# Layer 0's projection: when the second feature block's weights are loaded and split, which queue carries the modulation rows, and the form of the first modulation

## The chip, the cores and the metric

One core of a Trainium2 chip runs the whole kernel in one launch. The metric is the time of the launch in device microseconds (us); several launches of one kernel are timed and the median is taken. The engines are TensorE (PE in the rows; its weight loads are PEld), VectorE (DVE), ScalarE (ACT), GpSimd (POOL) and SyncE (SP), each with an instruction queue of its own that is worked off in order. DMAs are issued from such queues too, mostly SP's.

## The reference

Two layers over 1024 latent tokens and 256 context tokens of width 1024. Each layer modulates its input by rows that come from a condition vector (adaLN), runs an attention mixer, and then a gated FFN with a short convolution. Layer 0's projection, which matters here:

```python
m = split(silu(c) @ ada_w[l] + ada_b[l], 6)        # 6 modulation rows of 1024, for latent and context
h = x * (1 + m[1]) + m[0]
qa, ka, va, qb, kb, vb = split(h @ w_in, [512, 640, 768, 1280, 1792])
qa, ka = rms_norm per head, times gain, then axial rotary (latent tokens)
# group A: global attention; group B (qb, kb, vb, 8 heads each): neighbourhood attention
```

All is float32. A product is computed as three matmuls of a high and a low half (`mm3`): hi x hi, hi x lo, lo x hi.

## The kernel before

**Weights.** `load_in` brings a block of the weights from DRAM in loads of 512 KB into the pool `raw` (two buffers for the whole kernel) and calls `split`: ScalarE casts a tile to its high half (L99), VectorE subtracts for the low half (L100), both into a tile of the ring `ring` (12 slots). A block of 512 columns takes four loads and eight ring tiles, one for each 128 rows (k).

**First modulation** (`ada_first`, L141). While 8.4 MB of `ada_w` come in as 16 tiles `wt`, TensorE multiplies the two condition vectors with them, in pieces of 512 columns, into four PSUM banks; four strips of partitions hold partial sums that 32 small matmuls against the selector `sel` (L185; 16 in the code, each in two instructions) add up and turn into columns. Then `mod0` is built. x is loaded by `first_loads` behind the `wt` loads, then w_in, the rotary table `rope0` (L531) and the two gain rows (L138). `group(0, k)` transposes x (L512), applies the modulation on ScalarE (L514) and splits the result into the halves `hh` and `hl`.

**Token blocks** (`tok`): kA/vA, qA, then vB, with group by group of 24 matmuls for 128 tokens. Between them `conv_cols` loads rows of the convolution's weights into `rt` and transposes them to columns (L129), through the one bank `small`, which VectorE empties (L131). A generator `ada_items` (called by `bg`) is stepped in between as well: it loads modulation weights `araw`, accumulates them on VectorE (L215, L219) and sums them over the partitions with two matmuls (L309, L310).

**Feature blocks** (L684 on): `proj_feat` makes qB and then kB. For each of four f it takes three chunks of tokens (512, 512, 256), so twelve groups of 24 matmuls (L385 to L387) in each block. After each group `ev` evicts it (ScalarE and VectorE) to `qst`, stores it (L676), steps `bg(3)` and then `side`. `side` runs two parts of `ada_cols` one after the other: a part first issues its bias rows and its first load, then in eight steps loads the next 512 KB of layer 1's `ada_w` into `raw` (L274) and multiplies the one there into the bank `cols` (a set of eight matmuls, L289), then adds the bias (L299) and stores the rows to DRAM (L300). So the first part ends, and the second begins, in the tenth call, and two of the second part's sets lie in qB. kB's weights are loaded (L686) when qB's last group has been emitted.

After both blocks `mod_cols` (L692, L696) loads six rows each (two of the layer norm, four of modulation), transposes them to columns for `m1` and `m2`, and attention begins (L730).

**Order.** TensorE's instructions stand in the order of the code inside `manual_pe`. Those of the other engines, and all DMAs, are placed by a scheduler at build time, when it reckons that they are ready; at run time each queue keeps that order. A buffer that is taken again makes its writer wait for its last reader.

Of the kernel before, what the change touches and what calls it, by code (L numbers as in the profile page):

```python
# [36 lines left out]
class Kern:  # L37
# [66 lines left out]
    def load_in(self, w, c0, n, lo_eng=None):  # L104

        nc = self.nc
        wv = w.rearrange("(k p) n -> p k n", p=128)
        out = []
        g = 1024 // n
        for k0 in range(0, KT, g):  # L110
            r = self.t(self.raw, [128, g, n], "raw")
            nc.sync.dma_start(r, wv[:, k0 : k0 + g, c0 : c0 + n])
            for w2 in self.split([r[:, : g // 2], r[:, g // 2 :]], 512, lo_eng=lo_eng):
                v = w2.rearrange("p l (k n) -> p l k n", n=n)
                out += [(v[:, 0, k], v[:, 1, k]) for k in range(g // 2)]
        return out


    def cols(self, tp, ppool, rows, tag, pool=None):

        nc = self.nc
        n = sum(r.shape[0] for r in rows)
        rt = self.t(tp, [128, 128], "rt", bufs=3)
        o = 0
        for r in rows:
            nc.sync.dma_start(rt[o : o + r.shape[0], :], r)
            o += r.shape[0]
        ps = self.t(ppool, [128, 512], "small")
        nc.tensor.transpose(ps[:, :n], rt[:n, :], self.ident[:n, :n])  # L129
        ct = self.t(pool or self.cst, [128, n], tag)  # L130
        nc.vector.tensor_copy(ct, ps[:, :n])  # L131
        return ct
# [8 lines left out]
    def ada_first(self, loads):  # L141

        nc, io = self.nc, self.io
        with ExitStack() as es:
# [11 lines left out]
            ps = [self.t(pp, [128, 512], f"a{j}") for j in range(4)]  # L156
            for x in ps:
                nc.vector.memset(x, 0.0)
            ar = self.t(ap, [128, 2048], "ar")
            sel = self.t(ap, [128, 2], "sel")  # L160
            nc.vector.memset(sel, 0.0)
            for g in range(4):
                nc.vector.tensor_copy(sel[32 * g : 32 * g + 2], self.ident[:2, :2])
# [12 lines left out]
            loads()  # L176
            for j in range(4):
                d = ar[:, j * 512 : (j + 1) * 512]
                if j % 2:
                    nc.vector.tensor_copy(d, ps[j])  # L180
                else:
                    nc.scalar.copy(d, ps[j])
            pt = self.t(pp, [128, 512], "small")
            for j in range(16):
                nc.tensor.matmul(  # L185
                    pt[:, 2 * j : 2 * j + 2], ar[:, j * 128 : (j + 1) * 128], sel,
                    start=True, stop=True, skip_group_check=True,
                )
            m0 = self.t(self.cst, [128, 2, 8, 2], "mod0")
            nc.vector.tensor_add(  # L190
                m0.rearrange("p a k v -> p (a k) v"),
                pt[:, :32].rearrange("p (n v) -> p n v", v=2),
                ct[:, 16:32].unsqueeze(2).to_broadcast([128, 16, 2]),
            )
# [71 lines left out]
    def ada_cols(self, tp, bank, l, part):  # L266
# [11 lines left out]
        for c in range(4):  # L278
            b0 = part * D + c * 256
            nc.sync.dma_start(  # L280
# [187 lines left out]
    def l0_project(self):  # L468
# [11 lines left out]
        w = io["w_in0"]  # L480

# [9 lines left out]
        def first_loads():  # L491
            load_x(0, 0)
# [37 lines left out]
        rp = self.t(tab, [128, 8, 128], "rp")  # L530
        nc.sync.dma_start(rp, io["rope0"])  # L531
        gq = self.t(tab, [128, HD], "gq")
        gk = self.t(tab, [128, HD], "gk")
        self.bcast(gq, io["qg"][0])
        self.bcast(gk, io["kg"][0])
# [80 lines left out]
        with self.manual_pe():  # L616
# [32 lines left out]
            wb = None  # L649
            for t in range(NT):  # L650
                tok(t, wv, 512, ev_vb)
                bg(3)
# [7 lines left out]
        with ExitStack() as e3:  # L660
# [5 lines left out]
            side = (  # L666
                x for part in range(2)
                for x in self.ada_cols(colp, lambda: self.t(pc, [128, 512], "cols"), 1, part)
            )

            def ev_feat(dst, scale):
                def ev(f, t0, n, ps):
# [671 lines left out]
    def conv_cols(self, l, tp, pp):  # L1344
# [3 lines left out]
        c0 = self.cols(tp, pp, [cw[0], cw[1]], f"cc{l}0")  # L1348
        c1 = self.cols(tp, pp, [cw[2], cb], f"cc{l}1")
        return [c0[:, 0:NF], c0[:, NF:], c1[:, 0:NF], c1[:, NF:]]  # L1350
# [1037 lines left out]
```

## Time and profile before

| | us |
|---|---|
| median of 3 runs | 2991.7 (2990.74 to 2994.36) |
| profiled execution | 2995.48 |
| its span, first to last instruction | 2993.7 |
| busy: TensorE / VectorE / ScalarE / GpSimd | 2836.2 / 2046.6 / 1366.0 / 625.0 |
| share of the chain that ended last: TensorE / VectorE / DMA / ScalarE | 81% / 7% / 5% / 4% |
| mean granted clock of TensorE | 0.973 |

The page of the profile gives the busy time of each engine and the chain of work that ended last, followed back from the last instruction. A stretch of the span can be cut out: its busy times, the clock that TensorE was granted (1.00 is 2.4 GHz, 0.50 is 1.2 GHz) and the DMA engines' share. A timeline lists instructions in order of time: the start in us from the start of the span, the length, the engine (SPq is SP's DMA queue), the line, the tiles written and read, the count when several are merged, and in brackets the idle time before it and what ended that.

### The profile page before, as it was taken

What the parts mean: (1) busy time and instruction counts of PE and PEld (TensorE: products, weight loads), DVE (VectorE), ACT (ScalarE), POOL (GpSimd) and SP (SyncE); (2) the same over time, 40 slices, a digit from 0 to 9 for tenths busy, and PEclk for the clock granted to TensorE, in tenths of its full rate; (3) what the DMA queues carried; (4) which work ended last, traced back from release to release, by engine and by line L of the source; (5) the groups of instructions that cost most, each with busy time, mean ns of one, the idle gap of its engine ahead of it and who ended that gap; (6) DMA issues with size and microseconds to landing.
All of it is one profiled execution on the core that took longest, in us unless ns stands there. A gap on an engine that the chain in (4) does not pass through costs nothing.

```text
span 2993.7 us, 44874 instructions
## 1 busy us (share of the span) xinstructions
PE 2836.2 (95%) x16692; PEld 2291.7 (77%) x16692; DVE 2046.6 (68%) x3768; ACT 1366.0 (46%) x2595; POOL 625.0 (21%) x840
## 2 busy tenths in 40 slices
PE   8997899999999989999999988989997999999998
PEld 5875677777788978888888877766676788888886
DVE  4875266666578778888878655467776777777655
ACT  4221155567435654444553352167743545545330
POOL 2610033354450000000001013345543000000001
PEclk8998999999999999999999998999998999999999
DMA  7567521033557653333367526732154222224741
GB/s 256 154 214 231 169 81 35 17 101 113 159 150 239 211 161 104 109 106 116 106 231 275 167 75 215 205 102 64 60 162 160 76 80 83 80 85 156 266 146 73
DMA packets 348227, 418.58 MB, mean 140 GB/s; under 512 B 23128, under 2 KB 263032, under 8 KB 346472
## 3 DMA queue, kind: packets, MB, share of 16 engines
q1 hardware_dynamic: 330248, 361.30, 38.6%
q0 software_dynamic: 14864, 52.70, 5.0%
q8 instruction: 131, 2.15, 0.3%
q10 hardware_dynamic: 2896, 1.70, 0.2%
q14 instruction: 88, 0.72, 0.1%
HBM read 318.84 MB, written 96.80 MB: 139 GB/s over the span
## 4 chain that ended last, share of the span: by engine, by line
PE 81%; DVE 7%; DMA 5%; ACT 4%; issue 2%; POOL 1%; SPq 0%; ACTq 0%; POOLq 0%; DVEq 0%
PE y L1667 8%; PE q L1667 8%; PE x L1667 8%; PE d L385 5%; PE d L386 5%; PE d L387 5%; PE S L730 5%; PE v L1667 4%; PE mm L385 4%; PE mm L386 3%; PE mm L387 3%; PE pv L875 3%; PE T L861 3%; PE pv L835 2%; PE T L826 2%; PE o L387 2%
## 5 line engine op out<-in xcount | busy, mean ns | idle before, releaser
L754 POOL TENSOR_SCALAR P<-P,rin 128x640 f32<-128x640 f32 (+3 forms) x288 | 250.8, 875 | 350.4 <-DVE rin L753 315.9
L1566 DVE TENSOR_TENSOR w<-raw,w 128x512 fp32r<-128x512 f32 x308 | 208.8, 691 | 164.8 <-ACT w L1564 164.7
L385 PE MATMUL d<-w,w 128*128 128x512 f32 x704 | 275.2, 391 | 0.0
L387 PE MATMUL d<-w,w 128*128 128x512 f32 x704 | 274.4, 390 | 0.0
L386 PE MATMUL d<-w,w 128*128 128x512 f32 x704 | 274.4, 390 | 0.0
L99 ACT CAST w<-raw 128x512 fp32r<-128x512 f32 x276 | 160.9, 620 | 186.6 <-PE d L387 127.4
L100 DVE TENSOR_TENSOR w<-raw,w 128x512 fp32r<-128x512 f32 x260 | 170.4, 696 | 107.7 <-ACT w L99 105.4
L730 PE MATMUL S<-k,q 64*128 64x256 f32 (+2 forms) x1824 | 193.0, 338 | 17.5 <-DVE nm L2109 7.9
L1714 POOL DMA_DIRECT2D g<-cv x44 | 23.5, 533 | 870.0 <-DVE cv L1713 870.0
L751 ACT ACTIVATE P<-P,nm 128x641 f32<-128x641 f32 (+4 forms) x208 | 161.4, 777 | 82.9 <-DVE nm L2109 46.7
L1564 ACT CAST w<-raw 128x512 fp32r<-128x512 f32 x308 | 182.6, 621 | 15.2 <-DVE raw L1571 11.4
L730 PEld LDWEIGHTS S<-k,q 64*128 64x128 f32 x1824 | 136.2, 189 | 52.9 <-issue 17.6
L741 ACT COPY PT<-T 128x512 f32<-128x512 f32 (+1 forms) x250 | 134.1, 566 | 81.1 <-PE T L861 78.8
L387 PEld LDWEIGHTS d<-w,w 128*128 128x128 f32 x704 | 132.4, 188 | 27.9
L385 PEld LDWEIGHTS d<-w,w 128*128 128x128 f32 x704 | 132.6, 188 | 27.5
L386 PEld LDWEIGHTS d<-w,w 128*128 128x128 f32 x704 | 132.6, 188 | 27.1
L875 PE MATMUL pv<-PT,v 128*64 128x128 f32 x2016 | 134.7, 282 | 14.4 <-ACT PT L741 13.1
L1658 DVE TENSOR_TENSOR w<-raw,w 128x512 fp32r<-128x512 f32 x176 | 112.3, 686 | 52.0 <-ACT w L1657 51.9
L861 PE MATMUL T<-ident,P 128*128 128x128 f32 x1008 | 136.3, 282 | 12.0 <-POOL P L754 8.1
L1802 ACT COPY ug<-q 128x512 f32<-128x512 f32 x44 | 25.8, 587 | 254.8 <-PE q L1667 254.8
L875 PEld LDWEIGHTS pv<-PT,v 128*64 128x64 f32 x2016 | 110.6, 139 | 40.6 <-ACT PT L741 23.0
L1657 ACT CAST w<-raw 128x512 fp32r<-128x512 f32 x176 | 98.8, 618 | 87.2 <-PE d L387 70.1
(338 smaller groups left out, 7624.8 us busy)
## 6 DMA issues: line engine op xcount, KB each, us to landing
raw<-in_up_dram SPq DMA_DIRECT2D x132, 512.0 KB
raw<-g SPq DMA_DIRECT2D x88, 512.0 KB
raw<-in_down_dram SPq DMA_DIRECT2D x66, 512.0 KB
g<-cv POOLq DMA_DIRECT2D x44, 512.0 KB, 3.0
araw<-in_ada_w_dram SPq DMA_DIRECT2D x32, 512.0 KB
raw<-in_w_in_dram SPq DMA_DIRECT2D x28, 512.0 KB
araw<-in_ada_w_dram SPq DMA_DIRECT2D x40, 256.0 KB
wt<-in_ada_w_dram SPq DMA_DIRECT2D x16, 512.0 KB
```

What stands on the lines that cost most here:

```text
L100: (lo_eng or nc.vector).tensor_sub(lo, s, f32(hi))
L385: nc.tensor.matmul(ps, lh, rh, start=first, stop=False)
L386: nc.tensor.matmul(ps, lh, rl, start=False, stop=False)
L387: nc.tensor.matmul(ps, ll, rh, start=False, stop=last)
L730: self.nc.tensor.matmul(outs[a], q[r, x, qs], k[r, y, ks], start=(i == 0), stop=(i == 2))
L751: nc.scalar.activation(P[:, :m], P[:, :m], AF.Exp, bias=negm, scale=-1.0, accum_out=den)
L754: nc.gpsimd.tensor_scalar(P[:, :n], P[:, :n], rin, 1.0, ALU.mult, ALU.mult)
L861: nc.tensor.transpose(ps[:, s * 128 : (s + 1) * 128], P[a][:, cols[i + x] : cols[i + x] + 128], self.ident,)
L875: nc.tensor.matmul(O[a * HD : (a + 1) * HD], v_of(a, vts[i + x]), pT[:, s * 128 : (s + 1) * 128], start=(i + x == 0), stop=(i + x == m - 1 ...
L1564: nc.scalar.copy(half(i, 0), src[i])
L1566: nc.vector.tensor_sub(half(i, 1), src[i], f32(half(i, 0)))
L1667: nc.tensor.matmul(ps, w[:, a, s], r[b][:, k], start=first and k + i == 0, stop=k == 3 and i == 2, skip_group_check=True,)
```

## The change

- kB's weights are loaded in two halves (`load_in` takes `ks`): the first after qB's first group, the second after its eleventh, when the first part of `ada_cols` has been drained. The first part is stepped from the second group of qB on, the second from the second group of kB on.
- `ada_cols` issues its loads, bias rows and stores from GpSimd's queue.
- `ada_first` works in pieces of 256 columns in four strips, each with the full sum, into two banks; two copies and four transposes replace four copies and the selector matmuls, and two additions replace one.
- `rope0` and the gain rows are loaded ahead of x, into other pools.
- The convolution's rows are all loaded ahead of the last tiles of kA and transposed together after vB's first group. `cols` takes one `rt` buffer unless told otherwise (`conv_cols`: four) instead of three.

```diff
-    def load_in(self, w, c0, n, lo_eng=None):
+    def load_in(self, w, c0, n, lo_eng=None, ks=range(KT)):
...
-        for k0 in range(0, KT, g):
+        for k0 in ks[::g]:
...
-    def cols(self, tp, ppool, rows, tag, pool=None):
+    def cols_late(self, tp, ppool, rows, tag, pool=None, bufs=1):
...
-        rt = self.t(tp, [128, 128], "rt", bufs=3)
+        rt = self.t(tp, [128, 128], "rt", bufs=bufs)
...
+        def make():
+            ps = self.t(ppool, [128, 512], "small")
+            nc.tensor.transpose(ps[:, :n], rt[:n, :], self.ident[:n, :n])
+            ct = self.t(pool or self.cst, [128, n], tag)
+            nc.vector.tensor_copy(ct, ps[:, :n])
+            return ct
+
+        return make
+
+    def cols(self, tp, ppool, rows, tag, pool=None, bufs=1):
+        return self.cols_late(tp, ppool, rows, tag, pool, bufs)()
...
-            ps = [self.t(pp, [128, 512], f"a{j}") for j in range(4)]
+            ps = [self.t(pp, [128, 512], f"a{h}") for h in range(2)]
...
-                    for j in range(2):
-                        b = 2 * h + j
-                        g = (b + k) % 4
+                    for c in range(4):
                         nc.tensor.matmul(
-                            ps[b][32 * g : 32 * g + 2, :], self.cs[:, :, k],
-                            wt[:, j * 512 : (j + 1) * 512], start=k < 4, stop=k >= 4,
-                            tile_position=(0, 32 * g), skip_group_check=True,
+                            ps[h][32 * c : 32 * c + 2, :256], self.cs[:, :, k],
+                            wt[:, c * 256 : (c + 1) * 256], start=k == 0, stop=k == KT - 1,
+                            tile_position=(0, 32 * c), skip_group_check=True,
                         )
             loads()
+            ar = self.t(ap, [128, 2, 256], "ar")
+            nc.scalar.copy(ar[:, 0], ps[0][:, :256])
+            nc.vector.tensor_copy(ar[:, 1], ps[1][:, :256])
...
-            for j in range(16):
-                nc.tensor.matmul(
-                    pt[:, 2 * j : 2 * j + 2], ar[:, j * 128 : (j + 1) * 128], sel,
+                s = slice(j % 2 * 128, j % 2 * 128 + 128)
+                nc.tensor.transpose(
+                    pt[:, j * 128 : (j + 1) * 128], ar[:, j // 2, s], self.ident
+                )
...
-            nc.sync.dma_start(r, io["ada_w"][l][k * 128 : (k + 1) * 128, c0 : c0 + D])
+            nc.gpsimd.dma_start(r, io["ada_w"][l][k * 128 : (k + 1) * 128, c0 : c0 + D])
...
-            nc.sync.dma_start(self.d["ada"][l, :, part, c * 256 : (c + 1) * 256], br[s])
+            nc.gpsimd.dma_start(self.d["ada"][l, :, part, c * 256 : (c + 1) * 256], br[s])
...
         def first_loads():
+            nc.sync.dma_start(rp, io["rope0"])
+            self.bcast(gq, io["qg"][0])
+            self.bcast(gk, io["kg"][0])
             load_x(0, 0)
             load_x(0, 1)
...
-            conv = self.conv = []
+            conv = [self.conv_cols(l, st, pa) for l in range(2)]
...
-                if t in (5, 7):
-                    conv.append(self.conv_cols(len(conv), st, pa))
...
                 tok(t, wv, 512, ev_vb)
+                if t == 0:
+                    self.conv = [f() for f in conv]
...
+            side = [
+                self.ada_cols(colp, lambda: self.t(pc, [128, 512], "cols"), 1, part)
+                for part in range(2)
+            ]
...
                     bg(3)
-                    next(side, None)
+                    n_ev.append(0)
+                    then(len(n_ev))
...
+            def then1(i):
+                if i == 1:
+                    wb2.extend(self.load_in(w, 1280, 512, ks=range(4)))
+                if 2 <= i < 11:
+                    next(side[0], None)
+                if i == 11:
+                    for _ in side[0]:
+                        pass
+                    wb2.extend(self.load_in(w, 1280, 512, ks=range(4, 8)))
+
+            def then2(i):
+                if i >= 2:
+                    next(side[1], None)
...
-                self.proj_feat(pp, chunks, wb, ev_feat(d["qB"], HD ** -0.5))
-                wb = self.load_in(w, 1280, 512)
-                self.proj_feat(pp, chunks, wb, ev_feat(d["kB"], None))
-                for g in (side, ada[0]):
+                self.proj_feat(pp, chunks, wb, ev_feat(d["qB"], HD ** -0.5, then1))
+                self.proj_feat(pp, chunks, wb2, ev_feat(d["kB"], None, then2))
+                for g in (side[1], ada[0]):
```

## Rows read from the trace of the kernel before

**Rows 1.** Busy time by stretch; columns: stretch, length, engines, granted clock, DMA share, GB/s

```profile
206.00:278.40 72.40, 69.12 (x380) 52.59 (x379) 45.81 (x76) 9.96 (x19) 0.00 (x0) 0.98 0.73 232
278.40:310.90 32.50, 12.37 (x36) 7.28 (x40) 11.96 (x19) 5.41 (x10) 0.00 (x0) 0.55 0.80 234
```

**Rows 2.** Timeline of TensorE, 268 to 316; columns: start, us, instruction, idle before

```profile
280.53 0.62 PE L289 MATMUL cols<-raw,cs 128*2 128x256 f32 x8 [2.21 <-DMA raw<-in_ada_w_dram]
289.88 0.80 PE L385 MATMUL mm<-hh,w 128*128 128x512 f32 x1 [8.74 <-ACT w L99]
...
310.23 0.63 PE L387 MATMUL mm<-hh,w 128*128 128x512 f32 x1
```

**Rows 3.** Timeline of SP's queue, 230 to 311

```profile
280.67 0.49 SPq L274 DMA_DIRECT2D raw<-in_ada_w_dram  x1
281.26 0.44 SPq L112 DMA_DIRECT2D raw<-in_w_in_dram  x1
...
282.12 2.30 SPq L126 DMA_DIRECT2D rt<-ada  x4
...
291.27 0.39 SPq L112 DMA_DIRECT2D raw<-in_w_in_dram  x1
...
297.04 0.38 SPq L112 DMA_DIRECT2D raw<-in_w_in_dram  x1
```

**Rows 4.** Timeline of VectorE and ScalarE, 278 to 296

```profile
283.87 5.39 DVE L219 SCALAR_TENSOR_TENSOR acc<-araw,cs,acc 128x512 f32<-128x512 f32 x8 [4.68 <-DMA araw<-in_ada_w_dram]
...
295.07 1.14 ACT L99 CAST w<-raw 128x512 fp32r<-128x512 f32 x2 [4.72 <-DMA raw<-in_w_in_dram]
```

**Rows 5.** Timeline of ScalarE, 200 to 395: evictions of kB's groups

```profile
334.98 0.59 ACT L442 CAST qst<-mm 128x512 fp32r<-128x512 f32 x1 [5.76 <-PE mm L387]
338.56 0.37 ACT L442 CAST qst<-mm 128x256 fp32r<-128x256 f32 x1 [3.00 <-PE mm L387]
...
353.31 0.37 ACT L442 CAST qst<-mm 128x256 fp32r<-128x256 f32 x1 [2.25 <-PE mm L387]
...
367.36 0.37 ACT L442 CAST qst<-mm 128x256 fp32r<-128x256 f32 x1 [2.27 <-PE mm L387]
```

**Rows 6.** Groups by line and form, 206 to 367.4; columns: busy, mean | idle before

```profile
L289 PE MATMUL cols<-raw,cs 128*2 128x256 f32 x128 | 10.3, 394 | 5.4 <-DMA raw<-in_ada_w_dram 5.4
```

**Rows 7.** Timeline of all engines, 0 to 62

```profile
1.51 0.32 SPq L126 DMA_DIRECT2D rt<-in_ada_b_dram  x1
...
3.11 0.28 PE L129 MATMUL small<-ident,rt 32*128 32x32 f32 x1 [3.11 <-DMA rt<-in_ada_b_dram]
...
26.83 1.03 PE L171 MATMUL a<-wt,cs 128*2 128x512 f32 x4 [1.45 <-DMA wt<-in_ada_w_dram]
...
27.79 6.13 PE L185 MATMUL small<-sel,ar 128*128 128x2 f32 x32
...
29.20 0.34 SPq L531 DMA_DIRECT2D rp<-in_rope_dram  x1
...
33.77 6.41 PE L512 MATMUL tr<-ident,x 128*128 128x128 f32 x32
...
34.90 2.48 ACT L514 ACTIVATE sg<-tr,mod 128x512 f32<-128x512 f32 x3 [6.43 <-PE tr L512]
```

**Rows 8.** Busy time by stretch, columns as in the first group

```profile
24.50:29.50 5.00, 3.55 (x20) 1.81 (x17) 1.39 (x2) 1.17 (x2) 0.00 (x0) 0.93 1.06 268
```

**Rows 9.** TensorE's waits, 92 to 106: us in total, times, longest

```profile
PE small L129 <- DVE cc L131: 4.1, 2, 2.5
```

**Rows 10.** DMA issues: count, KB each, median us from issue to landing

```profile
araw<-in_ada_w_dram POOLq DMA_DIRECT2D x24, 256.0 KB, 5.5
```

**Rows 11.** Timeline of TensorE, 364.5 to 373

```profile
367.81 0.26 PE L129 MATMUL small<-ident,rt 48*128 48x48 f32 x1 [0.30 <-DVE m1c L131]
368.47 1.70 PE L730 MATMUL S<-k,q 64*128 64x256 f32 x24 [0.40 <-DVE m1ab L331]
```

**Rows 12.** Timeline of GpSimd, 90 to 395

```profile
358.99 1.07 POOL L1030 MEMSET E<- 128x256 f32 x4 [201.43 <-PE mm L387]
```

More of the change, by code (lines that the diff above doesn't have):

```diff
@@ L127, in cols @@
             o += r.shape[0]
[L128 to L132, printed above, removed]
+        def make():
[7 more added lines that the diff above has]
+        return self.cols_late(tp, ppool, rows, tag, pool, bufs)()
     def row128(self, ap):
@@ L155, in ada_first @@
             w = io["ada_w"][0].rearrange("(k p) n -> p k n", p=128)
-            ps = [self.t(pp, [128, 512], f"a{j}") for j in range(4)]
+            ps = [self.t(pp, [128, 512], f"a{h}") for h in range(2)]
             for x in ps:
[L158 to L163, printed above, removed]
+                nc.vector.memset(x[:, :256], 0.0)
             for k in range(KT):
@@ L175, in ada_first @@
                         )
             loads()
+            ar = self.t(ap, [128, 2, 256], "ar")
+            nc.scalar.copy(ar[:, 0], ps[0][:, :256])
+            nc.vector.tensor_copy(ar[:, 1], ps[1][:, :256])
+            pt = self.t(pp, [128, 512], "small")
             for j in range(4):
[L178 to L183, printed above, removed]
@@ L184, in ada_first @@
-            for j in range(16):
-                nc.tensor.matmul(
-                    pt[:, 2 * j : 2 * j + 2], ar[:, j * 128 : (j + 1) * 128], sel,
-                    start=True, stop=True, skip_group_check=True,
+                s = slice(j % 2 * 128, j % 2 * 128 + 128)
+                nc.tensor.transpose(
+                    pt[:, j * 128 : (j + 1) * 128], ar[:, j // 2, s], self.ident
                 )
             m0 = self.t(self.cst, [128, 2, 8, 2], "mod0")
[L190 to L194, printed above, removed]
+            for h in range(2):
+                nc.vector.tensor_add(
+                    m0[:, h].rearrange("p (c b) v -> p c b v", b=2),
+                    pt[:, h * 256 : (h + 1) * 256].rearrange(
+                        "p (b c v) -> p c b v", b=2, c=4
+                    )[:, :, :, :2],
+                    ct[:, 16 + 8 * h : 24 + 8 * h].rearrange(
+                        "p (c b) -> p c b", b=2
+                    ).unsqueeze(3).to_broadcast([128, 4, 2, 2]),
+                )
@@ L279, in ada_cols @@
             b0 = part * D + c * 256
-            nc.sync.dma_start(
+            nc.gpsimd.dma_start(
                 br[32 * c : 32 * c + 2], io["ada_b"][l, b0 : b0 + 256].partition_broadcast(2)
@@ L480, in l0_project @@
         w = io["w_in0"]
+        rp = self.t(xp, [128, 8, 128], "rp", bufs=1)
+        gq, gk = (self.t(self.cst, [128, HD], "g" + n) for n in "qk")
         def load_x(i, h):
@@ L529, in l0_project @@
         wk = self.load_in(w, 512, 256)
[L530 to L535, printed above, removed]
         nc.vector.tensor_scalar(gq, gq, HD ** -0.5, None, ALU.mult)
@@ L648, in l0_project @@
                 bg(3)
-            wb = None
             for t in range(NT):
                 tok(t, wv, 512, ev_vb)
+                if t == 0:
+                    self.conv = [f() for f in conv]
                 bg(3)
@@ L665, in l0_project, with ev_feat @@
             colp = e3.enter_context(self.pool("colp"))
[L666 to L671, printed above, removed]
+            side = [
+                self.ada_cols(colp, lambda: self.t(pc, [128, 512], "cols"), 1, part)
+                for part in range(2)
+            ]
+            def ev_feat(dst, scale, then):
+                n_ev = []
                 def ev(f, t0, n, ps):
@@ L677, in ev @@
                     bg(3)
-                    next(side, None)
-                return ev
+                    n_ev.append(0)
+                    then(len(n_ev))
+                return ev
+            wb2 = []
+            def then1(i):
[10 more added lines that the diff above has]
+                    next(side[1], None)
             chunks = [(H[0][0], H[0][1], 0, 512), (H[1][0], H[1][1], 512, 512),
@@ L1347, in conv_cols, with make @@
         cb = io["cb"][l].rearrange("(f p) -> f p", p=128)
-        c0 = self.cols(tp, pp, [cw[0], cw[1]], f"cc{l}0")
-        c1 = self.cols(tp, pp, [cw[2], cb], f"cc{l}1")
-        return [c0[:, 0:NF], c0[:, NF:], c1[:, 0:NF], c1[:, NF:]]
+        f = [
+            self.cols_late(tp, pp, r, f"cc{l}{i}", bufs=4)
+            for i, r in enumerate(([cw[0], cw[1]], [cw[2], cb]))
+        ]
+        def make():
+            c0, c1 = f[0](), f[1]()
+            return [c0[:, 0:NF], c0[:, NF:], c1[:, 0:NF], c1[:, NF:]]
+        return make
     def ctx_up(self, pu, ws, h):
```

## The prediction, made before the changed kernel was run

> **What bounds the kernel now.** I read the page first, its busy times and its chain of work that ended last: TensorE has nearly all of both, so only time in which TensorE stands still, or runs at its half clock, can be won. Next I cut the span into stretches and looked for one where its busy time falls. The hole lies between the two feature blocks of layer 0's projection (qB, then kB): from 278.4 to 310.9 us TensorE is busy for 12.37 of 32.5 us at a granted clock of 0.55 (mostly the lower of its two levels, 1.2 and 2.4 GHz), against 69.12 of 72.4 us at 0.98 in the stretch before it [rows 1]. TensorE's own instructions show its shape: a `cols` set runs at 280.53 after 2.21 us of waiting for its load, and then kB's first group of 24 matmuls starts at 289.88, after 8.74 us of waiting for ScalarE's split of a weight tile, and only ends near 310.9 [rows 2]. SP's queue shows why. The weights of kB are four loads into the two `raw` buffers: the first goes out at 281.26, right behind an `ada_cols` load (280.67) that takes the other buffer, and that one is freed only by a `cols` set that stands behind kB's first group. So the other three go one at a time, the first of them at 291.27, the next at 297.04: load, split, release, load [rows 3]. There are three such rounds, some 5.8 us each. VectorE adds to the first round: eight accumulations take 283.87 to 289.3 after 4.68 us of waiting for `araw`, and the low halves of the split stand behind them; in a later round ScalarE waits 4.72 us for the data [rows 4].
>
> What would this cost without holes? ScalarE's evictions mark the ends of groups: 353.31 to 367.36 is three undisturbed groups (512, 512 and 256 columns), 14.05 us; by their columns one of 512 takes 5.62 and one of 256 takes 2.81. From 334.98 to 338.56 a small group with one `cols` set before it takes 3.58, so a set costs 0.77 [rows 5].
>
> **The change, part by part.**
>
> *Half of kB's weights a block ahead, `side` cut in two.* After qB's first group two loads (four weight tiles) go into `raw` and into the four ring slots that wb doesn't hold (12 slots, wb has 8). The first part of `ada_cols` runs from the 2nd to the 11th group and is drained there; only then come the other two loads, with both `raw` buffers free. Their splits wait for ring slots of wb's first four tiles, which the 12th group releases one by one. The hole between 278.4 and 310.9 is 32.5 us, of which one group (5.62) and one set (0.77) are work: **-26.1 us**. What is late next? kB's fifth weight tile. Its slot is free about 0.35 us into the 12th group (an eighth of 2.81), so 2.5 us before kB; it is needed after four tiles, half a group, 2.8 us into kB. That leaves 5.3 us for a cast and a subtraction, whose pace in the rows is two casts in 1.14 us [rows 4]; the loads can go out at the latest sets of `side`, one and two groups earlier. I take **0**, with an upper bound of +7 (second rival).
>
> *Work that only moves.* Sixteen `cols` sets stay sixteen (8 and 8 instead of 10 and 6). All sets together waited 5.4 us for their loads [rows 6], 2.2 of it in the hole [rows 2], so 3.2 elsewhere. Those loads now go through GpSimd's queue, which sat idle for 201.43 us up to 358.99 [rows 12], so they no longer stand behind SP's stores, each with its own wait for a split result. The nearest price of a load on that queue is 5.5 us from issue to landing for 256 KB [rows 10], half the bytes of ours. Load k+1 is released by set k-1 and needed by set k+1: two groups, at least 2.81 + 5.62 = 8.43 us. It fits, but kB's four loads (2.1 MB) now partly share qB's DMA time, where queues moved 232 GB/s at a share of 0.73 [rows 1]. Bounds: -4.2 (all waits and the half clock after them gone) to +4 (waits doubled). I take **-1.0**, nearer to the gain, since 5.5 lies well under 8.43.
>
> The Trainium skill speaks against this queue ("SBUF — State Buffer", section "SBUF: two separate sides"): descriptors of DMAs that GpSimd issues can't be written while VectorE runs an instruction that takes both ports. By that rule alone these loads would land late whenever VectorE is in such an instruction; by its own condition accumulations with two tensor inputs are not of that kind, and no run here shows the price yet. The first rival below is worked out without it.
>
> *First modulation in quarters.* Before: the last set of the modulation's matmuls starts at 26.83 and takes 1.03; then 32 small matmuls from 27.79 for 6.13 us gather the columns; ScalarE's first use is at 34.90 [rows 7], 1.0 us after them. After: eight 256-column pieces of the `cols` form (busy 10.3 us in 16 sets, 0.64 each [rows 6]) end at 27.5; two copies of half the width side by side, 0.37 as ScalarE's 256-column eviction [rows 5], 27.9; four transposes at 6.41/32 = 0.20 each [rows 7], 28.7; the additions as before 1.0, plus a second one, some 29.9 instead of 34.9. But then x is late. `rope0` (0.52 MB) and the two gain rows now stand ahead of x in SP's queue, where `rope0` was issued at 29.20, behind x [rows 7]. The queues are full: 268 GB/s from 24.5 to 29.5 [rows 8]. Half of x (1.05 MB) takes 3.9 us, so it was there at about 29.6; 0.52 MB ahead adds 2.0 and the gain rows some 0.3: 31.9, and four transposes 0.8: 32.6 instead of 34.9. **-2.3 us**, with bounds 0 (the table products on GpSimd, now earlier, disturb VectorE there) and -5.0 (x not late).
>
> *The convolution's columns.* Loads early, four transposes in a row after the first token tile of vB. They share one PSUM buffer, so each waits for VectorE's copy of the one before. Before, two such waits cost 4.1 us, the longer one 2.5 [rows 9]; after, three waits at one spot, with the data long there: 3 x 0.3 to 3 x 2.5. Bounds -3 to +3; I take **0**.
>
> *One `rt` buffer where there were three.* `cols` now asks for one buffer, and the two `mod_cols` after kB share the tag. The second one's six row loads must wait for the first one's transpose, which stands behind kB's last matmul. Now the second transpose starts at 367.81 after 0.30 us of waiting for the copy, and the first attention matmuls at 368.47 [rows 11]. After: six issues on SP at 2.30/4 = 0.58 [rows 3], the last 2.9 us on; from issue to the transpose that needs it 1.6 us (1.51 to 3.11 [rows 7]); 4.5 instead of 0.3: **+4.2 us**, before attention, whose chain starts there. SP's kB stores and q loads queue behind the six issues, too, but are needed later. Bounds 0 (attention's matmuls are put ahead of the transpose) and +5.
>
> Sum: -26.1 + 0 - 1.0 - 2.3 + 0 + 4.2 = **-25.2 us**. The profiled execution took 2995.48 us (span 2993.7, and 1.8 around it); it lies 3.8 us (0.13%) above the median of 2991.7, so I subtract from the median: **2966.5**.
>
> **The rivals.**
> 1. *Slower: GpSimd's loads arrive late.* Two of three steps have 8.43 us. When a load takes L us, 11 of the 16 sets wait L - 8.43 each. The 25.2 us are gone at L = 10.7; at 11.5 it is 11 x 3.07 = 34 us of waiting, **3000**. Against it: 5.5 us in the nearest row, half of that. 4%.
> 2. *The second half of the weights is late.* VectorE works in order; with another `araw` wait ahead of the splits as at 283.87 (4.68 + 5.39 = 10.1 us of wait and work [rows 4]) plus 1.3 for the split against 5.3 of room, TensorE stands still for 6 us and has half its clock for about 1 more: **2973**. For it: the same generator still feeds VectorE at that point. 20%.
> 3. *The end doesn't wait.* The first attention matmuls go ahead of the second transpose, or the row loads find their buffer earlier: **2962**. 20%.
> 4. *It does not do what it says.* If one `raw` buffer stays taken, the last two loads still go one by one, two rounds of 5.8 us less 2.8 of cover: **2975**. 8%.
> 5. No change within 0.2% by some other cost of 20 us: 3%.
>
> **How the numbers follow.** My own case has 45%, in 2963 to 2970. The range must take in cases 2 to 4 and the bounds of the small terms (start 2.3 more or less, `cols` waits up to 4 more, 3 less): **2957 to 2978**. A measurement of this kernel tells 0.2%, 6 us, from no change. Faster by more: 0.94; within: 0.03; slower: 0.03.
>
> **What would show it.** Right: kB's first group takes 5.6 to 6.5 us right behind qB, at a clock of 1.0; kB's four loads are issued in pairs, the first pair near qB's first group; kB's last eviction comes about 29 us before 367.36, near 338. ScalarE's first modulated tile starts near 32.6. At the end the two small transposes stand 4 to 5 us apart. Wrong: `cols` sets that wait for POOL's loads in most groups; a wait for ScalarE's or VectorE's split at kB's fifth tile; a first modulated tile at 34 or later; second transposes within 1 us.

## The result, and the profile of the changed kernel

The changed kernel takes 2964.9 us (median; 2964.4 to 2965.9), the kernel before 2992.2 beside it: a ratio of 0.9909, with a 95% interval of 0.9891 to 0.9926, so 27 us faster (22 to 33). The profiled execution has a span of 2963.4 us. The time that I gave, 2966.5, is 1.6 us off; what follows shows that it came out of terms that were wrong in both directions.

The hole between the feature blocks, first. Busy time by stretch, columns as in [rows 1] (length; TensorE, its weight loads, VectorE, ScalarE, GpSimd; granted clock, DMA share, GB/s): qB up to its last eviction, the 19.5 us behind it, and the rest of kB.

```profile
213.00:283.20 70.20, 67.41 (x369) 51.79 (x369) 46.97 (x77) 14.01 (x27) 6.57 (x12) 0.98 0.86 275
283.20:302.70 19.50, 18.14 (x96) 14.59 (x95) 11.35 (x19) 3.01 (x7) 3.69 (x7) 1.00 0.95 271
302.70:347.00 44.30, 44.07 (x259) 33.34 (x257) 7.88 (x15) 4.66 (x10) 5.86 (x13) 1.00 0.63 195
```

Where [rows 1] had 12.37 busy of 32.5 us at a clock of 0.55, there are now 18.14 of 19.5 at 1.00. SP's queue and ScalarE show how; they answer [rows 3] and [rows 4, 5]:

```profile
215.03 1.58 SPq L112 DMA_DIRECT2D raw<-in_w_in_dram  x2
...
271.03 0.38 SPq L112 DMA_DIRECT2D raw<-in_w_in_dram  x1
...
277.64 0.38 SPq L112 DMA_DIRECT2D raw<-in_w_in_dram  x1
```

```profile
279.78 1.14 ACT L99 CAST w<-raw 128x512 fp32r<-128x512 f32 x2 [0.22 <-PE mm L390]
282.12 1.14 ACT L99 CAST w<-raw 128x512 fp32r<-128x512 f32 x2 [1.20 <-DMA raw<-in_w_in_dram]
...
287.85 0.59 ACT L445 CAST qst<-mm 128x512 fp32r<-128x512 f32 x1 [4.30 <-PE mm L390]
...
346.61 0.37 ACT L445 CAST qst<-mm 128x256 fp32r<-128x256 f32 x1 [2.27 <-PE mm L390]
```

The first pair of kB's loads goes out in qB's first group. The second pair goes one by one, and the last split begins at 282.12, just as kB's first group does (its first matmul stands at 282.07, its eviction at 287.85: 5.78 us, at a clock of 1.00). kB's last eviction is at 346.61 instead of 367.36.

The modulation's sets on GpSimd's queue [rows 6], as a group of 213 to 347, and the start [rows 7]:

```profile
L292 PE MATMUL cols<-raw,cs 128*2 128x256 f32 x128 | 10.3, 393 | 4.1 <-DMA raw<-in_ada_w_dram 4.1
```

```profile
29.11 0.17 DVE L198 TENSOR_SCALAR mod<-mod 128x16 f32<-128x16 f32 x1
30.30 0.48 PE L520 MATMUL tr<-ident,x 128*128 128x128 f32 x1 [1.52 <-DMA x<-in_x_dram]
...
33.35 3.69 PE L520 MATMUL tr<-ident,x 128*128 128x128 f32 x16 [0.52 <-DMA x<-in_x_dram]
33.86 2.48 ACT L522 ACTIVATE sg<-tr,mod 128x512 f32<-128x512 f32 x3 [7.63 <-PE tr L520]
```

The modulation is ready at 29.3, and the first tile waits for x until 33.86 (34.90 before).

The row of small transposes behind vB's first tile, where [rows 9] had two waits of 4.1 us in all; TensorE's timeline, and busy time by stretch:

```profile
149.71 0.29 PE L132 MATMUL small<-ident,rt 88*128 88x88 f32 x1 [2.26 <-DVE abr L317]
153.40 0.41 PE L132 MATMUL small<-ident,rt 88*128 88x88 f32 x1 [3.39 <-DVE cc L134]
154.82 0.41 PE L132 MATMUL small<-ident,rt 88*128 88x88 f32 x1 [1.01 <-DVE cc L134]
155.67 0.41 PE L132 MATMUL small<-ident,rt 88*128 88x88 f32 x1 [0.45 <-DVE cc L134]
156.52 0.77 PE L312 MATMUL small<-ahl,ones 128*128 128x512 f32 x1 [0.44 <-DVE cc L134]
```

```profile
150.00:154.00 4.00, 0.42 (x2) 0.18 (x1) 4.00 (x9) 2.11 (x4) 4.00 (x1) 0.79 0.60 188
154.00:158.00 4.00, 2.30 (x6) 1.59 (x7) 3.22 (x9) 0.00 (x0) 0.91 (x1) 0.50 0.71 188
158.00:162.00 4.00, 4.00 (x11) 3.14 (x10) 3.08 (x5) 0.00 (x0) 0.00 (x0) 0.50 1.00 341
```

VectorE is busy for 4.00 of 4.00 us; each transpose waits for its copy of the one before, which stands in its full queue, and the clock is 0.50 behind it. vB's first tile ends at 147.45 (149.71 less the wait of 2.26) and the second is evicted at 165.58, 18.1 us later, where one tile is 6.5 us of work: 11.6 us lost at one spot, against 6.0 us that the two pairs cost in kA before (two gaps of 5.3 and 7.3 us between tiles that else stand 3.3 apart).

Last, the start of the attention [rows 11, 12]:

```profile
346.51 0.26 PE L132 MATMUL small<-ident,rt 48*128 48x48 f32 x1
347.68 1.70 PE L749 MATMUL S<-k,q 64*128 64x256 f32 x24 [0.92 <-PE small L132]
351.52 0.23 PE L132 MATMUL small<-ident,rt 48*128 48x48 f32 x1 [2.14 <-DMA rt<-ada]
...
365.30 0.33 PE L880 MATMUL T<-ident,P 128*128 128x128 f32 x1 [0.66 <-POOL P L773]
366.65 1.42 PE L880 MATMUL T<-ident,P 128*128 128x128 f32 x11 [1.02 <-POOL P L773]
```

The second small transpose does stand 5.0 us behind the first, but the S products went ahead of it: attention starts 20.8 us earlier, exactly as kB's end does. Behind it something happened that the prediction didn't have. In the kernel before, GpSimd's order in the first attention block is P, E, P, E (the scaling of P, then the bias E, two instructions that wait for their own data and stand as x2 in the rows), and TensorE waits for the second P; in the changed kernel it is P, P, E, E. The order is fixed when the kernel is built, and edits elsewhere flip it: six of the fourteen kernels here have P, E, P, E, and TensorE waits 2.9 to 3.8 us for the second P in them; in the eight others (P, P, E, E, or P, P, P, E with the halves on SyncE's queue) it waits 1.0 us or less. The kernel before, GpSimd and TensorE, then GpSimd of the changed one:

```profile
384.42 1.33 POOL L754 TENSOR_SCALAR P<-P,rin 128x1280 f32<-128x1280 f32 x1 [8.47 <-PE S L730]
387.12 1.94 POOL L1064 TENSOR_TENSOR E<-G,msk 128x384 f32<-128x384 f32 x2 [1.37 <-DVE y L991]
389.04 1.33 POOL L754 TENSOR_SCALAR P<-P,rin 128x1280 f32<-128x1280 f32 x1
390.42 2.61 PE L861 MATMUL T<-ident,P 128*128 128x128 f32 x11 [3.75 <-POOL P L754]
```

```profile
363.91 2.68 POOL L773 TENSOR_SCALAR P<-P,rin 128x1280 f32<-128x1280 f32 x2 [8.76 <-DVE rin L772]
366.73 1.96 POOL L1083 TENSOR_TENSOR E<-G,msk 128x384 f32<-128x384 f32 x2
```

By 400 us the changed kernel is 24.7 us ahead: 3.9 more than at the attention's start.

### The profile page after: what moved, and what is told of

Same layout as the page of the kernel before. It is cut to its first block, busy times and chain, and to the rows that moved or that the text cites. A ratio compares the mean times of both kernels' runs of the same rounds, so it can differ in the third digit from the quotient of the medians.

```text
span 2963.4 us, 44978 instructions
## 1 busy us (share of the span) xinstructions
PE 2812.4 (95%) x16728; PEld 2276.9 (77%) x16728; DVE 2052.6 (69%) x3761; ACT 1365.3 (46%) x2594; POOL 636.9 (21%) x872
## 4 chain that ended last, share of the span: by engine, by line
PE 76%; DVE 8%; DMA 7%; ACT 5%; issue 2%; POOL 1%; SPq 0%; ACTq 0%; DVEq 0%; POOLq 0%
PE y L1693 8%; PE q L1693 8%; PE x L1693 8%; PE d L389 5%; PE d L390 5%; PE d L388 5%; PE S L749 4%; PE v L1693 4%; PE pv L894 3%; PE T L880 3%; PE mm L388 2%; PE mm L389 2%; PE mm L390 2%; ACT P L770 2%; PE o L390 2%
## 5 line engine op out<-in xcount | busy, mean ns | idle before, releaser
L390 PEld LDWEIGHTS d<-w,w 128*128 128x128 f32 x704 | 132.1, 188 | 27.2
L1828 ACT COPY ug<-q 128x512 f32<-128x512 f32 x44 | 25.9, 588 | 253.7 <-PE q L1693 253.7
```

What stands on the lines that cost most here:

```text
L390: nc.tensor.matmul(ps, ll, rh, start=False, stop=last)
```

## The experiments

All times are medians with their ratio to the kernel before, run beside them. "qB starts" is its first matmul, "blocks" the time from there to kB's last eviction (the expectations count them from the end of vB's last sums, some 0.9 us later: 132.8 there is 133.8 here).

| kernel | us | ratio, 95% interval | qB starts | kB ends | blocks |
|---|---|---|---|---|---|
| before | 2992.2 | | 207.69 | 367.36 | 159.67 |
| changed | 2964.9 | 0.9909 (0.9891 to 0.9926) | 212.82 | 346.61 | 133.79 |
| halves_only | 2957.7 | 0.9887 (0.9871 to 0.9904) | 207.18 | 336.11 | 128.93 |
| halves_gpsimd | 2969.5 | 0.9922 (0.9909 to 0.9934) | 204.22 | 338.51 | 134.29 |
| second_load_sync | 2963.8 | 0.9912 (0.9896 to 0.9928) | 208.00 | 338.10 | 130.10 |
| sp_queue | 2963.1 | 0.9906 (0.9891 to 0.9920) | 212.02 | 340.40 | 128.38 |
| conv_row_only | 2998.7 | 1.0019 (1.0010 to 1.0028) | 213.04 | 370.99 | 157.95 |
| conv_spread | 2966.1 | 0.9914 (0.9899 to 0.9929) | 208.44 | 339.70 | 131.26 |
| conv_back | 2966.4 | 0.9916 (0.9901 to 0.9931) | 206.06 | 340.96 | 134.90 |
| conv_back_sync | 2960.4 | 0.9893 (0.9879 to 0.9908) | 207.93 | 335.85 | 127.92 |
| conv_late_sync | 2958.4 | 0.9886 (0.9871 to 0.9901) | 203.68 | 334.48 | 130.80 |
| quarters_only | 2988.5 | 0.9985 (0.9975 to 0.9995) | 204.43 | 360.03 | 155.60 |
| rows_one_buffer | 2990.1 | 0.9988 (0.9979 to 0.9996) | 207.77 | 366.44 | 158.67 |
| rt_two_buffers | 2971.0 | 0.9931 (0.9916 to 0.9946) | 210.22 | 343.27 | 133.05 |

**The halves alone**, in the kernel before (then1, then2 and the cut of the side work as in the change, everything else as before):

```diff
-    def load_in(self, w, c0, n, lo_eng=None):
+    def load_in(self, w, c0, n, lo_eng=None, ks=range(KT)):
...
+                if i == 1:
+                    wb2.extend(self.load_in(w, 1280, 512, ks=range(4)))
...
+                    wb2.extend(self.load_in(w, 1280, 512, ks=range(4, 8)))
```

> The kernel before with one part alone: kB's weights in two halves, a block ahead, and the side work cut in two; its loads stay on SP's queue, all else is as before. Theory: the hole of 26.1 us closes, and since the order of GpSimd's queue at the start of attention comes out with the softmax scaling ahead of the bias products, about 3 more: 2963 (2960 to 2967), no part of it from the queue. Rival (it is GpSimd's queue that lets the loads be in time): the hole closes only in part, 2970 or more.

Measured: 2957.7 us, 5 us below what I expected; this part alone gains more than the whole change (34 us by its ratio). The blocks are 30.7 us shorter, and the sets wait for 0.8 us in all, by the group of 206 to 337:

```profile
L289 PE MATMUL cols<-raw,cs 128*2 128x256 f32 x128 | 9.8, 379 | 0.8 <-DMA raw<-in_ada_w_dram 0.8
```

**The queue.** Three issues in the changed kernel, of which the first is shown (the others load the bias rows and store the result), and the same three the other way in the halves alone:

```diff
-            nc.gpsimd.dma_start(r, io["ada_w"][l][k * 128 : (k + 1) * 128, c0 : c0 + D])
+            nc.sync.dma_start(r, io["ada_w"][l][k * 128 : (k + 1) * 128, c0 : c0 + D])
```

> The changed kernel, but the loads, bias rows and stores of the modulation rows are issued from SP's queue as before. Theory (the queue is worth next to nothing: the sets wait 4.1 us for their loads in the changed kernel and waited 5.4 in the one before): within 3 us of the changed kernel, 2962 to 2968. Rival (the queue carries the gain): 2970 or more. Second rival (descriptors that GpSimd writes come late): 2961 or less.

> The kernel before with the halves of kB's weights and the cut of the side work (as in the run with the halves alone, 2957.7 us), and the modulation's loads moved to GpSimd's queue; start and convolutions' columns as before. GpSimd's order at the first attention block is that of the kernel before. Theory (the queue costs some 5 us in the feature blocks, the order another 3 to 7 behind): qB and kB together take 131 to 134 us where the halves alone had 128.0, the waits for the modulation's weights are 4 to 5 us in place of 0.8, and the whole is 2966 to 2970 us. Rival (the queue costs nothing by itself, and the cost in the changed kernel comes from its other parts): 128 us, and 2958 to 2963 us.

Both agree on the blocks: 5.4 us longer with GpSimd's queue (133.79 against 128.38, 134.29 against 128.93). In the whole, SyncE's queue gives the changed kernel only 1.8 us, within the spread; its lead of 6.2 us at kB's end has shrunk to 3.2 by the end (spans of 2963.4 and 2960.2); GpSimd's queue costs the halves 10.5 by the ratios, of which some 3 are the order P, E, P, E that comes with this build (its wait for P is 3.54 us); the rest was lost step by step up to 2000 us, which I didn't follow up.

In the halves the 5.4 us lie at one place (in the changed kernel 4.5 lie there and 2.0 at kB's first set, and 1.1 come back elsewhere). SP's and GpSimd's queues, TensorE, and busy time by stretch in the kernel with the halves on GpSimd's queue:

```profile
213.96 0.48 SPq L726 DMA_DIRECT2D k<-kA  x1
214.44 0.67 POOL L274 DMA_DIRECT2D raw<-in_ada_w_dram  x1 [59.14 <-DVE w L100]
215.95 0.56 POOL L274 DMA_DIRECT2D raw<-in_ada_w_dram  x1 [0.84 <-DVE w L100]
...
222.89 1.04 PE L289 MATMUL cols<-raw,cs 128*2 128x256 f32 x8 [3.53 <-DMA raw<-in_ada_w_dram]
```

```profile
218.00:223.00 5.00, 1.47 (x14) 1.03 (x16) 3.07 (x5) 0.39 (x1) 0.00 (x0) 0.92 0.98 306
223.00:229.00 6.00, 6.00 (x20) 4.10 (x13) 0.00 (x0) 0.00 (x0) 0.54 (x1) 0.50 0.96 351
```

The first set of qB has its load 8.45 us after the issue (7.76 in the changed kernel: 222.99 to 230.75, with a wait of 2.79), TensorE stands still for 3.53, and the granted clock is 0.50 for the six us behind it. On SyncE's queue the first load stands alone for 6 us, since the second one waits there behind qB's stores. SyncE's own order changes too: rid of these loads, its queue sends a load of k for the attention (640 KB) 0.48 us ahead of the first one, in all five kernels that have both loads on GpSimd's queue. In the four that have them on SyncE's, that load of k goes out 74 to 80 us behind it.

**The second load on the other queue** (halves on GpSimd's queue otherwise):

```diff
-            nc.gpsimd.dma_start(r, io["ada_w"][l][k * 128 : (k + 1) * 128, c0 : c0 + D])
+            (nc.sync if k == 1 else nc.gpsimd).dma_start(
+                r, io["ada_w"][l][k * 128 : (k + 1) * 128, c0 : c0 + D]
+            )
```

> The kernel with the halves and GpSimd's queue (start and convolutions as before), with one edit: the second 512 KB of each modulation's part goes back to SyncE's queue, so that the first one is alone in GpSimd's at its start. GpSimd's order at the attention is unchanged. Theory (the queue's cost in the blocks is one wait of 3.5 us for the first 512 KB, which shares the DMA engines with the second that GpSimd issues 1.5 us behind it, and the half clock after that wait): the wait falls below 1.5 us, the clock stays at 1.0, the fourth eviction of qB comes 22 to 24 us after its start in place of 27.9, qB and kB take 129 to 131 us in place of 134.3, and the whole is 2964 to 2967 us in place of 2969.5. Rival (the queue by itself brings the first load late): the wait stays at 2.5 us or more with the half clock behind it, and the whole is 2968 to 2971 us.

GpSimd's and SP's queues, TensorE, and busy time by stretch:

```profile
218.29 0.67 POOL L274 DMA_DIRECT2D raw<-in_ada_w_dram  x1 [59.21 <-DVE w L100]
...
219.23 0.33 SPq L274 DMA_DIRECT2D raw<-in_ada_w_dram  x1
...
226.00 0.48 SPq L728 DMA_DIRECT2D k<-kA  x1
...
224.05 0.61 PE L291 MATMUL cols<-raw,cs 128*2 128x256 f32 x8 [0.91 <-DMA raw<-in_ada_w_dram]
```

```profile
227.00:233.00 6.00, 6.00 (x32) 4.27 (x31) 3.26 (x6) 0.60 (x1) 0.54 (x1) 1.00 1.04 288
```

The numbers came as the theory had them, the whole within 0.2 us (wait 0.91, clock 1.00, blocks 130.1; the whole, 2963.8, is 3.0 us below the halves on GpSimd's queue by the ratios, which is within the spread). But the edit moved two things: the second load, which now goes out 0.94 us behind the first on the other queue, and the load of k, which stands 7.7 us behind the first instead of 0.48 us ahead of it. This run can't tell the two apart.

Other rows of the traces speak for the load of k. At kB's border the same five kernels issue two loads 0.55 us apart on GpSimd's queue. The first of them lands 10.3 to 11.8 us after its issue, and its set waits (1.36 to 2.00 us), in the three where a load of k goes out just ahead of it; the changed kernel is one of them. In the two where that load goes out behind it, it lands after 4.4 us (the kernel with the halves on GpSimd's queue) and 5.4, and no set waits. In qB the late load also starts late: behind the issue at 214.44 no packet of GpSimd's queue moves for 3.8 us, while SyncE's packets take 104% of the DMA engines' time by the profile's count; behind the one at 218.29 the first packet moves after 1.6 us, with SyncE's at 79%. So it is most likely k's load, with which the first one shares the DMA engines, and not the second load beside it. No run moved k's load alone: this is read from the rows, not tested.

**The row of transposes.** Alone in the kernel before:

```diff
-                if t in (5, 7):
-                    conv.append(self.conv_cols(len(conv), st, pa))
...
+                if t == 0:
+                    self.conv = [f() for f in conv]
```

> The kernel before with the convolutions' columns alone moved: their rows loaded ahead of kA's second part, and the four small transposes in a row behind the first token tile of vB. GpSimd's order is that of the kernel before. Theory (the row costs 11.6 us at vB, and 6.0 us are won at kA): vB ends 4 to 6 us later than in the kernel before (208.8 us), and the whole is 2995 to 2998 us. Rival (the row costs no more than the pairs, as forecast): vB ends near 208.8 us and the whole is 2990 to 2993 us.

Measured: qB starts 5.35 us later, as the theory had it, and the whole is slower by 5.7 us (3.0 to 8.4), with the same waits (3.39 for the second transpose). In the changed kernel the row was taken apart, and taken back to its pairs:

```diff
-                if t == 0:
-                    self.conv = [f() for f in conv]
+                if t in (2, 4, 6, 8):
+                    got.append(conv[t // 2 - 1]())
```

> The changed kernel, but the four transposes of the convolution's columns stand one each behind vB's groups 2, 4, 6 and 8 (counted from 0) instead of all four behind group 0. Theory (the four in a row each wait for VectorE's copy, 2.26, 3.39, 1.01 and 0.45 us in the trace, and the half clock after it costs the next group about 4.7 us; 18.1 us between the two evictions, 151.35 and 165.58, and the end of the group before at 147.4, where 6.5 are work): each copy now has a whole group of time, so about 10 us are won, 2955 (2953 to 2958). Rival (VectorE's backlog is the cause and would stop TensorE a little later at the next partition sum, whose bank is the same): less than 4 us are won, 2961 or more.

> The changed kernel, but the convolution's columns are transposed where the kernel before had it, two behind the sixth and two behind the eighth tile of kA; the rows are still loaded early. Theory: the pairs cost there what they cost before, 6.0 us (the gaps of 5.3 and 7.3 us among tiles of 3.3), instead of 11.6 at vB, so 5 to 6 us are won, 2959 (2957 to 2961). Rival (place does not matter, it is the queue of VectorE that is late either way): 2963 to 2967.

Both theories missed, by 11 and 7 us (2966.1 against 2955, 2966.4 against 2959). Spread over vB, the row's loss falls by 4.4 us at qB's start (1.0 of it from a faster start), no more: the waits come back at the partition sums (3.6 us for VectorE's copies, 2.4 for its additions), as VectorE is full there either way. Back in pairs, qB starts 6.8 us earlier (1.1 from the start), and yet kB ends only 5.65 earlier, the sets having waited longer in these blocks (5.3 us). Neither gain shows in the whole. With SyncE's queue as well, pairs in kA and, in a second kernel, one transpose each behind kB's groups 6 to 9:

```diff
+                if i in (6, 7, 8, 9):
+                    got.append(conv[i - 6]())
```

> The changed kernel with the convolutions' columns made in pairs behind two tiles of kA, as in the kernel before, and the modulation's loads on SyncE's queue. What is left of the change is the start in quarters, the loads of the rotation's tables ahead of x, and the halves of kB's weights. Theory (the two costs add): vB ends near 207 us, qB and kB together take 127.5 us, kB's last eviction is near 334.6 us, some 1.5 us ahead of the run with the halves alone (336.1 us, the start's share), and the whole is 2955 to 2958 us. Rival (what is won ahead of the attention is given back behind it, as in the runs that moved one of the two alone): kB ends near 335 us all the same, but the whole is 2961 to 2965 us.

> The changed kernel with two edits: the modulation's loads go back to SyncE's queue, and the four small transposes of the convolutions' columns, which stand in a row behind the first token tile of vB, are made one each behind the groups 6 to 9 of kB, where VectorE has idle time. Theory (the row of four at vB costs 11.6 us less 6.0 us won at kA, GpSimd's queue some 5.4 us in the feature blocks, and both are free of each other): vB ends near 203 us instead of 213.8, qB and kB together take some 127.5 us instead of 132.8, the last eviction of kB is near 331 us instead of 346.6, and the whole is near 2951 us. Rival (VectorE is full at vB, so that what the transposes give back is waited for at the partition sums, as in the run that spread them over the tiles): vB ends near 208 us, kB near 336 us, and the whole is near 2957 us, as with the halves alone.

In the first of them the two costs add, near what was expected at kB's end (335.85 against 334.6), and the whole, 2960.4, lies between theory and rival. In the second, qB does start 4.3 us earlier, with a wait of 2.4 us for VectorE left at a sum, and the blocks take 2.9 us more for the transposes; the whole, 2958.4, is the rival's number. By 820 us the halves alone, the pairs and the late transposes are 37.7, 36.9 and 37.7 us ahead of the kernel before, though their attention started 31.3, 31.6 and 32.9 ahead: what is won above the halves ahead of the attention is gone by then. Which wait takes it I didn't find.

**The start** in quarters alone, in the kernel before, with the rotation's tables still behind x:

```diff
-            ps = [self.t(pp, [128, 512], f"a{j}") for j in range(4)]
+            ps = [self.t(pp, [128, 512], f"a{h}") for h in range(2)]
...
-            for j in range(16):
+            for j in range(4):
...
+                nc.tensor.transpose(
+                    pt[:, j * 128 : (j + 1) * 128], ar[:, j // 2, s], self.ident
+                )
```

> The kernel before with the first modulation in quarters of columns alone (two banks, four transposes in place of sixteen products with the selector); the tables of the rotation stay behind x, and nothing else is changed. Theory: the first modulated tile is 3 to 5 us earlier than in the kernel before (34.9 us), as x then stands ahead of the tables, but the first blocks of kA and qA wait for VectorE and give back all but some 2 us; the whole is 2988 to 2991 us. Rival (the start is carried through in full): 2986 to 2987 us.

Measured: a gain of 4.5 us (1.5 to 7.5), the theory's. The first modulated tile is at 32.85, with x waited for as well. In that execution the modulation's own weights came late: its last matmul starts at 28.95, against 26.91 in the changed kernel. x is there 3.4 us behind that matmul, and 5.7 to 6.4 us behind it in the seven kernels with the tables ahead of x, so the tables cost x 2.3 to 3.0 us, near the 2.3 that I had priced. With that, little is won at the first tile: it stands at 30.8 to 34.9 in the six kernels with the old start (median 33.4), at 32.9 to 33.9 in these seven (median 33.3). ScalarE's first square of a projected tile is a later mark, and it moves between executions of one and the same start: 49.86, 48.91, 49.66, 48.91, 47.50 and 45.04 in the six kernels with the old start, 46.3 to 47.4 in the eight with the new one; medians 48.9 and 46.6.

**The buffer for the rows, and GpSimd's order.** Two buffers in the changed kernel, and one buffer in the kernel before:

```diff
-        ct = self.cols(tp, pp, rows, tag + "c")
+        ct = self.cols(tp, pp, rows, tag + "c", bufs=2)
```

> The changed kernel with a second buffer for the rows of the last modulation's columns, so that its six loads no longer wait for the first small transpose; by this GpSimd's order at the first attention block is again that of the kernel before (one P, the two E, the other P). Theory (the gain of some 4 us behind the attention's start came from that order, and the wait for the one buffer costs nothing as the S products go ahead of it): kB ends at 346.6 us as in the changed kernel, PE waits again 3 to 4 us for P in the first block's ramp, and the whole is 2966 to 2968 us, against 2965. Rival (the forecast's: the one buffer costs up to 4 us of the attention's start): the attention starts 2 to 4 us earlier and the whole is 2961 to 2963 us.

> The kernel before with one edit: one buffer in place of three for the rows of the last modulation's columns. Its work is the same; by this edit alone GpSimd's order at the first attention block becomes that of the changed kernel (both P, then both E, where the kernel before has P, E, P, E). Theory (the order is what saves time behind the attention's start): PE's wait of 3.75 us for the second P becomes about 1 us, the wait of 2.66 us for the first P may go too as the S products go ahead of the second small transpose, and the whole is 4 to 7 us below the kernel before, near 2986.5 us. Rival (the forecast's term: the one buffer delays the attention by up to 4.2 us, and the order is worth nothing): 2992 to 2996 us.

The second buffer brings nothing at the attention's start (S products 1.06 us behind kB's last eviction, 1.07 with one), and the waits for P return: 2.71 and 3.40 us. Its lead of 3.3 us at kB's end is gone by 400 us, and the whole is 6.6 us slower by the ratios (2971.0, where I expected 2966 to 2968). The other way round, one buffer in the kernel before takes these waits away, as the second line below shows beside the 3.75 us above, and gains 3.6 us (1.2 to 6.3), a little less than the 4 to 7 of the theory. That it is the order and not the buffer by itself, two kernels with three buffers show: the halves alone (P, P, P, E) are 31.3 us ahead of the kernel before at the attention's start and 34.3 by 400 us, the halves on GpSimd's queue (P, E, P, E) 28.9 and 28.8. TensorE with two buffers in the changed kernel, then with one in the kernel before:

```profile
365.43 2.61 PE L880 MATMUL T<-ident,P 128*128 128x128 f32 x11 [3.40 <-POOL P L773]
```

```profile
387.85 1.42 PE L861 MATMUL T<-ident,P 128*128 128x128 f32 x11 [1.02 <-POOL P L754]
```

## Why the prediction was right, point by point

- **The hole (-26.1) and the waits of the sets (-1.0)**: right in kind and nearly in size. The blocks fell by 25.9 us, against 27.1 in the sum; with SyncE's queue they fall by 30.7, which is the hole and nearly all of the waits (5.4 to 0.8 us).
- **GpSimd's queue (in the -1.0)**: mis-sized. I priced a load by its median, 5.5 us, and that is what the median of the new ones is (5.5). But the sum goes by the first load of a block, which isn't released by a set two groups ahead: it is issued 10 us into qB and is wanted 5 us later. It took 7.8, and the first one of kB 10.3. I had counted the move only as a relief from SP's stores, and left out what SyncE's queue sends in the place that came free: a load of k, just ahead of these. Cost against the other queue: 5.4 us in the blocks. The first rival came true there, at two sets of sixteen (2.79 and 1.36 us) instead of eleven. The rule of the Trainium skill that I weighed ("SBUF — State Buffer", section "SBUF: two separate sides") would have loads late whenever VectorE takes both ports. The runs don't bear it out as the cause: the wait went from 3.53 to 0.91 us with the first load on the same queue and the same work on VectorE, and in the changed kernel two loads issued at 239.58 and 263.06, with VectorE busy without a pause, move their first packets after 1.6 and 1.7 us, as the one at 312.10 does (1.6) with VectorE idle for most of it.
- **The start (-2.3)**: -2.5 in the profiled pair and -2.3 by the medians above, at ScalarE's first square. At the first tile, for which I had worked it out, the medians show nothing (33.3 and 33.4): in the changed kernel it was 1.3 us later than forecast (33.86 against 32.6), as x landed until 33.35, and the 34.90 that I started from is the latest of six executions. What gains 2.3 us behind it isn't known, so that this size came out is partly luck.
- **The convolutions' columns (0)**: the term that failed. I priced three waits by [rows 9], but left out that VectorE is full at the new spot, and the half clock behind it. +5.35 us alone, above my bound of +3.
- **One buffer for the rows (+4.2)**: failed, and the third rival is what happened: the S products go ahead, and the cost is 0.
- **Not in the sum**: -3.9 us in the first attention block, some 3 of them by GpSimd's order, which came with the one buffer that I had priced as a loss.
- **The signs**: kB's first group (5.78 us at a clock of 1.00) came as I wrote; of the two pairs of loads only the first did; kB's last eviction, 346.6 instead of 338, showed the row and the queue before any experiment did; the first tile, at 33.86, lies just short of the 34 that I had called wrong; the small transposes stand 5.0 us apart, but with the S products between them, which I hadn't thought of as a sign.
- **The second rival** (second half late) did not come true, by little: the last split starts 0.05 us after kB's first matmul and is needed three quarters of a group (4.2 us) later, and VectorE's last subtraction for it ends at 285.83, 1.1 us before that tile's first matmul.

By the ratios, the parts alone give -33.8 (halves), +10.5 (GpSimd's queue), +5.7 (row), -4.5 (start) and -3.6 (one buffer): -25.7, against 27.2 us measured. Each of these is uncertain by 2.5 to 6 us. My 25.2 were as close by luck: errors of +6.6 (blocks 1.2, row 5.4) and -8.1 (buffer 4.2, first attention block 3.9) stood beside each other.

## What to carry to other kernels

Split the reload at a block's border so that half of it lies a block ahead: that one part made more than the whole gain, and a kernel with it alone (2957.7 us) beats the changed one. Price a load on another queue by the first one of a block, not by the median, and look at what the old queue then sends ahead of it. Price a row of small transposes by how full the engine is that copies them out. And look at the order on an engine shared by two chains (GpSimd's P and E) after any edit, even one that has nothing to do with it: some 3 us hung on it at that place, 3.6 and 6.6 us of the whole in the two runs that flipped it.

## What the runs showed of the hardware that I had not expected

- A 512 KB load on GpSimd's queue landed 8.45 us after its issue where a 640 KB load on SyncE's queue had gone out 0.48 us ahead of it; no packet of GpSimd's queue moved for the first 3.8 us. In the same kernel the first of two such loads 0.55 us apart landed after 4.4 us, with SyncE's load 1.0 us behind it.
- Behind a wait of 3.53 us TensorE's granted clock was 0.50 for six us, so that wait and clock cost 5.4 us in the blocks; behind one of 0.91 us at the same place it stayed at 1.00.
- One and the same start of the program ends anywhere between 45.0 and 49.9 us (ScalarE's first square), twice what the change was to win there.
